# Second mixer: gate products on four quarters of the array, ScalarE in program order, one head left for the tile-by-tile end

## The chip, the core and the metric

The kernel runs on one core of a Trainium2 chip. The metric is the device time in microseconds of one execution. A core has TensorE (PE in the profile, its weight loads apart as PEld), VectorE (DVE), ScalarE (ACT), GpSimd (POOL) and SyncE (SP), each with a queue of its own that is worked off in order. SP's queue issues the DMAs of the weights. Matmuls write to PSUM; the other operands live in SBUF.

## The reference, cut to what matters

Two layers work on 256 context tokens and 256 latent tokens of width 1024: a half-step SwiGLU, a token mixer, a second half-step SwiGLU, each between RMS norms. The change is in the token mixer of the second layer, where only the latent tokens go on:

```
a, bx per head (64 channels) and direction d:
  r = sigmoid(xc @ w_r[d] + b_r[d]);  i = sigmoid(xc @ w_i[d] + b_i[d])
  a = exp(-8 r softplus(-lam));       bx = sqrt(1 - a^2) * (i * xc)
h = linear scan of (a, bx), context first, then latent; d = 1 runs backwards
o_lru = gelu(gate) * (h[0] + h[1])                      512 channels
o_sc  = b * conv3(c * x)                                256 channels
o_cm  = gelu(u) * (w_s @ gelu(v) + b_s)                 256 channels
x = x + mod * rms_norm(concat(o_lru, o_sc, o_cm) @ w_mix_out)
```

The 8 heads are taken two by two: a group c of 128 channels holds two heads, so there are four groups, 0 to 3.

## The kernel before

Channels lie on the 128 partitions, tokens along the free dimension: context tokens in columns 0 to 255, latent tokens in columns 256 to 511. A big product is made three times with operands split in two fp32r parts: `split` (line 169) makes the high part with a cast on ScalarE (L173) and the low part with a subtraction on VectorE (L174), in two halves for each weight unit. The weights come by `load_split` through 4 raw tiles; the high and the low parts have 6 tiles each.

`mixer` (line 630) runs once for each layer. In the second layer (`len(segs) == 1`) the string `ORDER[1]` says in which order its parts are issued. A part is a letter and a number, looked up in the table `parts` (line 846): `c`, `x`, `b` are the three projections of the short convolution; `g` a gate projection with its gelu; `u`, `v`, `m` the chunk mixing; `w` the load of a slice of the output weights; `C`, `G`, `D`, `S` the four steps of a group of LRU heads: convolution (`conv`, line 697: one ScalarE instruction, L701, and three on VectorE, L703), gates (`lru_gates`, line 712), decay (`lru_decay`, line 726: exp L730 and tanh L731 on ScalarE for each direction, then L732, L734, L735 on VectorE), scan (`lru_scan`, line 738: a square root on ScalarE, L741, for each direction, the rest on VectorE up to L751). `p` is the output product of slice m with the four short-convolution and chunk parts (k = 4 to 7).

Within the block at line 874 TensorE keeps the order of the program (`MANUAL`); the other engines' instructions are placed by the scheduler of the language, which may pull one ahead of another. A projection takes its weights from a queue that is loaded two units ahead (`unit`, line 675), so the two casts of a unit are issued two projections before its product.

`lru_gates` multiplies, for each direction, the block-diagonal 128x128 weights of two heads (half of them zeros) with all 512 columns of the group's convolution output: four fp32 products of 128x512 for each group, each in one PSUM bank. A sigmoid on ScalarE empties each bank (L719, L723). PSUM tiles named mm come from a pool of 6 banks (line 91), which go round.

The output product (`out_mm`, line 833) is plain fp32: for each slice m of 128 output channels it adds up eight products 128x256, k = 0 to 3 for the LRU groups, 4 to 7 for the others. `LATE` splits the LRU groups: for those of `LATE[0]` the products of all eight slices are made one group after the other (`out_part`, line 842); those of `LATE[1]` are made slice by slice at the end, and after each slice `tile_sums` (line 891) takes it up: three ScalarE instructions (L899 to L901) and a product and sums on VectorE and GpSimd, whose column sums TensorE makes with a vector of ones (tiles st). L934 reads them when all are done; the norm's scale and the next FFN follow. In this last part `MANUAL2` keeps the order of TensorE and VectorE; casts for the next FFN's weights (`pieces`) stand between the slices.

## Time and profile before

| | us |
|---|---|
| median of 3 runs (lowest, highest) | 1643.89 (1642.16, 1644.5) |
| the profiled execution | 1642.21 |
| its span, first to last instruction | 1640.4 |
| PE busy in it | 1612.5 (98%) |
| DVE busy | 1164.3 (71%) |
| ACT busy | 736.7 (45%) |
| POOL busy | 120.3 (7%) |

Times within the trace are microseconds from the span's start. The second mixer's parts run from about 1351 to 1439, so it is some 90 us of the whole. In a timeline row the first number is the start, the second the length from the start of the row's first instruction to the end of its last, and the bracket at the end is idle time of that engine just before, with what ended it. Instructions of an engine overlap a little, so the step from one to the next is shorter than one alone takes. The busy share of an engine over the whole run says little here, since the mixer uses the engines in other proportions than the FFNs around it.

### The profile page before, as it was taken

The page shows a single profiled execution, that of the slowest core. Times are in us where ns is not written, and L with a number is a line of the kernel's source. Part 1 is how long each engine was busy: PE and PEld are TensorE (multiplying, and loading weights), DVE is VectorE, ACT ScalarE, POOL GpSimd, SP SyncE. Part 2 cuts the span into 40 slices and gives each one's busy share as a digit, 9 for nine tenths or more (in the row PEclk, how much of TensorE's full clock was granted, in tenths as well). Part 3 has the DMA queues.
Part 4 walks back from the last instruction along what each step waited for, and adds up shares of the span by engine and source line. Part 5 has one row for each costly group of instructions (what it writes and reads, how often), then busy time and mean ns, then how long its engine had stood idle before and what let it go on. Part 6 is the DMA issues. An engine that isn't in the chain of part 4 may idle for free.

```text
span 1640.4 us, 23432 instructions
## 1 busy us (share of the span) xinstructions
PE 1612.5 (98%) x8846; PEld 1371.6 (84%) x8846; DVE 1164.3 (71%) x2183; ACT 736.7 (45%) x1378; POOL 120.3 (7%) x166
## 2 busy tenths in 40 slices
PE   6999999999999999999999999999999999999998
PEld 3788888889977998888888998888888998789997
DVE  4899898548788787867763887767432788785554
ACT  5523322244697662332233462332232479864543
POOL 0000000005000500000000410000000410100000
PEclk9999999999999999999999999999999999999999
DMA  9577677431323225655552215655422316155552
GB/s 370 189 218 261 205 229 223 144 121 44 103 72 120 77 97 187 221 162 174 179 164 80 100 61 194 222 166 167 141 90 90 103 54 210 47 167 194 180 191 78
DMA packets 73906, 249.97 MB, mean 152 GB/s; under 512 B 8384, under 2 KB 10048, under 8 KB 73792
## 3 DMA queue, kind: packets, MB, share of 16 engines
q1 hardware_dynamic: 73216, 247.94, 45.9%
q8 instruction: 69, 1.13, 0.3%
q10 hardware_dynamic: 576, 0.52, 0.1%
q14 instruction: 45, 0.37, 0.1%
HBM read 247.39 MB, written 1.05 MB: 151 GB/s over the span
## 4 chain that ended last, share of the span: by engine, by line
PE 89%; DVE 6%; ACT 3%; DMA 1%; issue 1%; POOL 0%; SPq 0%; POOLq 0%; DVEq 0%; ACTq 0%
PE mm L113 87%; PE st L113 1%; DVE x L271 1%; DVE sq L394 1%; DVE t L703 0%; PE mod L113 0%; DVE z L270 0%; DVE tmp L262 0%; DMA x<-in_xT 0%; ACT hi L173 0%; DVE t L397 0%; POOL rs L241 0%; DVE t L332 0%; DMA raw<-in_w_mi 0%; ACT t L730 0%
## 5 line engine op out<-in xcount | busy, mean ns | idle before, releaser
L173 ACT CAST hi<-raw 128x512 fp32r<-128x512 f32 (+1 forms) x596 | 343.6, 610 | 672.7 <-PE mm L113 475.8
L113 PE MATMUL mm<-hh,hi 128*128 128x512 f32 (+1 forms) x1840 | 625.6, 348 | 0.5 <-ACT hh L1095 0.2
L113 PE MATMUL mm<-hl,hi 128*128 128x512 f32 (+1 forms) x1840 | 622.5, 346 | 1.8 <-DVE hl L256 1.0
L174 DVE TENSOR_TENSOR lo<-raw,hi 128x512 fp32r<-128x512 f32 (+1 forms) x596 | 387.5, 680 | 157.3 <-ACT hi L173 154.5
L113 PE MATMUL mm<-hh,lo 128*128 128x512 f32 (+1 forms) x1840 | 466.6, 346 | 0.0
L113 PEld LDWEIGHTS mm<-hh,hi 128*128 128x128 f32 x1840 | 345.5, 188 | 52.1 <-ACT hh L1095 2.8
L113 PEld LDWEIGHTS mm<-hl,hi 128*128 128x128 f32 x1840 | 345.9, 188 | 51.2 <-DVE hl L1101 1.6
L113 PEld LDWEIGHTS mm<-hh,lo 128*128 128x128 f32 x1840 | 325.1, 188 | 47.2
L196 DVE SCALAR_TENSOR_TENSOR junk<-raw,cb 128x1024 bf16<-128x1024 f32 x256 | 312.9, 1222 | 70.8 <-DMA raw<-in_w_mod 67.1
L113 PE MATMUL mm<-t,hi 128*128 128x512 f32 (+1 forms) x1056 | 240.6, 367 | 0.0
L113 PEld LDWEIGHTS mm<-t,hi 128*128 128x128 f32 x1056 | 182.8, 188 | 35.7 <-issue 0.2
L397 POOL TENSOR_TENSOR t<-t,sq 128x256 f32<-128x256 f32 x112 | 94.2, 856 | 712.2 <-ACT sq L391 702.3
L113 PE MATMUL mm<-t,lo 128*128 128x512 f32 (+1 forms) x528 | 131.5, 367 | 0.0
L113 PEld LDWEIGHTS mm<-t,lo 128*128 128x128 f32 x528 | 92.6, 188 | 17.7
L480 DVE TENSOR_TENSOR sg<-sg,mm 128x512 f32<-128x512 f32 (+1 forms) x72 | 45.9, 640 | 78.3 <-PE mm L113 78.3
L113 PE MATMUL mm<-t,hh 128*128 128x256 f32 x512 | 71.2, 281 | 0.0
L113 PEld LDWEIGHTS mm<-t,hh 128*128 128x128 f32 x512 | 65.7, 188 | 0.5
L173 ACT CAST t<-sg 128x512 fp32r<-128x512 f32 (+1 forms) x94 | 50.6, 541 | 32.0 <-DVE sg L480 29.0
L332 DVE TENSOR_TENSOR t<-t,mm 128x256 f32<-128x256 f32 (+1 forms) x66 | 35.4, 536 | 29.3 <-PE mm L113 29.1
L174 DVE TENSOR_TENSOR t<-sg,t 128x512 fp32r<-128x512 f32 (+1 forms) x94 | 55.3, 589 | 0.9 <-ACT t L173 0.9
L113 PE MATMUL mm<-hi,t 128*128 128x512 f32 x176 | 55.1, 394 | 0.0
L263 ACT ACTIVATE hh<-tmp,modv 128x256 fp32r<-128x256 f32 x72 | 42.4, 596 | 22.1 <-DVE tmp L262 21.9
(179 smaller groups left out, 1212.4 us busy)
## 6 DMA issues: line engine op xcount, KB each, us to landing
raw<-in_w_in SPq DMA_DIRECT2D x176, 512.0 KB, 3.6
raw<-in_w_mod SPq DMA_DIRECT2D x128, 512.0 KB, 4.3
raw<-in_w_out SPq DMA_DIRECT2D x48, 512.0 KB, 3.3
raw<-in_w_mi SPq DMA_DIRECT2D x36, 512.0 KB, 4.1
raw<-in_w_last SPq DMA_DIRECT2D x22, 512.0 KB, 3.3
raw<-in_w_out SPq DMA_DIRECT2D x24, 384.0 KB, 3.7
t<-in_w_mod SPq DMA_DIRECT2D x32, 256.0 KB, 5.8
raw<-in_w_mo SPq DMA_DIRECT2D x8, 512.0 KB, 3.7
```

What stands on the lines that cost most here:

```text
L113: te.matmul(dst, lhsT=lhsT, rhs=rhs, start=start, stop=stop)
L173: sc.copy(hi, src)
L174: ve.tensor_tensor(lo, src, hi.bitcast(F32), op=OP.subtract)
L196: ve.scalar_tensor_tensor(junk, raw.rearrange("p k c -> p (k c)"), 1.0, cb[:, s], op0=OP.mult, op1=OP.mult, accum_out=modv[l][:, v, m, s:s ...
L263: sc.activation(hh[:, m, a:b], tmp, AF.Identity, scale=A, bias=B)
L271: ve.scalar_tensor_tensor(x[:, m, a:b], z, mcol(l, 3 * i + 2, m, s), x[:, m, a:b], op0=OP.mult, op1=OP.add)
L332: ve.tensor_tensor(y[m][:, a:b], y[m][:, a:b], p[:, :b - a], op=OP.add)
L394: ve.scalar_tensor_tensor(q[2], y, G, x[:, m, a:b], op0=OP.mult, op1=OP.mult)
L397: (gp if JACC[c] == "g" else ve).tensor_tensor(acc[c], acc[c], q[c], op=OP.add)
L480: ve.tensor_tensor(sg[:, :b - a], sg[:, :b - a], pu[:, :b - a], op=OP.mult)
```

## The change

Four things change, all in the second layer's mixer but for one name.

1. `lru_gates` works with 64x64 blocks. Each of the four products of a group becomes two products of 64 rows by 64 columns; the four that belong to one direction lie on the four quarters of the array. For this the convolution output is also needed with its two halves of partitions exchanged: `lru_swap` copies it with two DMAs of 128 KB from GpSimd's queue. The weights come in four small DMAs for a group instead of one of 256 KB. The first mixer keeps its products; its weight tile has another name.
2. ScalarE joins the engines that keep the program's order in the block of the parts.
3. `ORDER[1]` groups the parts by function.
4. `LATE` goes from `((0,), (1, 2, 3))` to `((1, 0, 3), (2,))`: groups 1, 0 and 3 are multiplied for all slices first, only group 2 is left for the slice-by-slice end.

```diff
-LATE = ((0,), (1, 2, 3))
+LATE = ((1, 0, 3), (2,))
...
-         "c0 x0 C1 C0 C3 C2 g3 g2 G1 G0 D1 D0 c1 b0 u0 v0 S1 w0 G3 u1 x1 b1 m1 w1 S0 m0 G2 w2 p1 w3 w4 w5 p2 p5 w6 D2 S2 w7 p0 "
-         "D3 S3 p7 p4 p3 p6")
+         "c0 x0 C1 C0 C3 C2 g3 g2 G1 G0 c1 b0 D1 D0 u0 u1 v0 S1 w0 S0 G3 G2 x1 b1 m1 m0 w1 w2 D3 D2 p1 w3 w4 w5 p2 p5 w6 S3 S2 w7 p0 "
+         "p7 p4 p3 p6")
...
+        def lru_swap(c):
+            t = turned_xc[c] = tp.tile([P, T], F32, tag="swap", name=nm("swap"), bufs=2)
+            for a, b in ((0, P // 2), (P // 2, 0)):
+                gp.dma_start(t[a:a + P // 2], xcs[c][b:b + P // 2])
+
+        def gate_products(c):
...
+            if len(segs) == 1:
+                wbd = tp.tile([P, 2, 2, P // 2], F32, tag="wbd", name=nm("wbd"))
+                for g in range(2):
+                    for h in range(2):
+                        a = 64 * h
+                        src = w_lru[l, c].rearrange("p (d g) o -> p d g o", g=2)
+                        nc.sync.dma_start(wbd[64 * g:64 * g + 64, :, h], src[a:a + 64, :, g, a:a + 64])
...
+            def products(d):
+                ps2 = pbank(), pbank()
+                for g, p in enumerate(ps2):
...
+                    for h in range(2):
+                        src = (xcs if g == h else turned_xc)[c]
+                        rows, cols = slice(64 * g, 64 * g + 64), slice(64 * h, 64 * h + 64)
+                        pe.matmul(p[cols], lhsT=wbd[rows, d, h], rhs=src[rows], start=True, stop=True)
+                return ps2
...
-                pr = pbank()
-                pe.matmul(pr, lhsT=wbd[:, 2 * d, :], rhs=xcs[c], start=True, stop=True)
+                pr, pi = products(d)
...
-        with tc.manual_schedule(engines=MANUAL):
+        with tc.manual_schedule(engines=MANUAL | {mybir.EngineType.Activation}):
```

What moves on the queues, at the three places that matter. First ScalarE, between the decays of groups 1 and 0 and the next gates (L730, L731 before are L764, L765 now; L805 is L839, the gelu of u; L798 is L832, the gelu of v; L741 is L775, the square root; L719 and L723, the sigmoids, are L755 and L757; L173 casts weights). Before:

```order
L805 ACT_TABLE_LOAD
L805 ACTIVATE t_12287<-mm_12262 128x256
L741 ACT_TABLE_LOAD
L741 ACTIVATE t_12125<-t_12125 128x512
L798 ACT_TABLE_LOAD
L798 ACTIVATE t_12330<-mm_12305 128x256
L741 ACT_TABLE_LOAD
L741 ACTIVATE t_12134<-t_12134 128x512
L798 ACT_TABLE_LOAD
L798 ACTIVATE t_12330<-mm_12332 128x256
L719 ACT_TABLE_LOAD
L719 ACTIVATE t_12373<-mm_12371,vec 128x512
```

and now, from the last instruction of the decays on:

```order
L765 ACTIVATE t_12182<-t_12182,s_100 128x512
L173 CAST hi_12282<-raw_12280 128x512 x2
L839 ACT_TABLE_LOAD
L839 ACTIVATE t_12313<-mm_12288 128x256
L173 CAST hi_12317<-raw_12315 128x512 x2
L839 ACTIVATE t_12348<-mm_12323 128x256
L173 CAST hi_12352<-raw_12350 128x512 x2
L173 CAST hi_12360<-raw_12358 128x512 x2
L832 ACTIVATE t_12391<-mm_12366 128x256
L832 ACTIVATE t_12391<-mm_12393 128x256
L775 ACT_TABLE_LOAD
L775 ACTIVATE t_12144<-t_12144 128x512
```

Fifteen table loads stand on ScalarE between the convolutions and the tile-by-tile end before, seven now. The casts of the two weight units of v (hi_12282 and hi_12317) now stand behind all eight instructions of the decays, and the square roots behind the second gelu of v.

Second TensorE, the gates of group 1 (wbd holds the gate weights, t_12031 the convolution output, swap its exchanged copy, each mm one PSUM bank). Before, four products, and the first of group 0:

```order
L113 MATMUL mm_12123<-t_12031,wbd_12121 128x512
L113 MATMUL mm_12127<-t_12031,wbd_12121 128x512
L113 MATMUL mm_12132<-t_12031,wbd_12121 128x512
L113 MATMUL mm_12136<-t_12031,wbd_12121 128x512
L113 MATMUL mm_12143<-t_12036,wbd_12141 128x512
```

Now on the same queue, with the swapped copy as one of the sources, all four of the first direction and the first of the second:

```order
L113 MATMUL mm_12138<-t_12031,wbd_12133 64x512
L113 MATMUL mm_12138<-swap_12036,wbd_12133 64x512
L113 MATMUL mm_12139<-swap_12036,wbd_12133 64x512
L113 MATMUL mm_12139<-t_12031,wbd_12133 64x512
L113 MATMUL mm_12149<-t_12031,wbd_12133 64x512
```

The second product of each group already needs the swapped copy. The gates of groups 3 and 2 now stand directly behind one another, eight banks in a row; before, five projections and a chunk mixing lay between them.

Third TensorE at the end (t_12134, t_12519 and t_12382 are the results of groups 1, 2 and 3 before; t_12461 and t_12488 those of groups 3 and 2 now; wo the output weights, one tile for each slice; c the product whose column sums st takes). Before:

```order
L113 MATMUL mm_12539<-t_12134,wo_12526 128x256
L113 MATMUL mm_12539<-t_12519,wo_12526 128x256
L113 MATMUL mm_12539<-t_12382,wo_12526 128x256
L113 MATMUL st_12635<-ones,c_12645 128x2 x2
L113 MATMUL mm_12539<-t_12134,wo_12533 128x256
L113 MATMUL mm_12539<-t_12519,wo_12533 128x256
L113 MATMUL mm_12539<-t_12382,wo_12533 128x256
L113 MATMUL st_12635<-ones,c_12651 128x2 x2
```

and now:

```order
L113 MATMUL mm_12639<-t_12461,wo_12633 128x256
L113 MATMUL mm_12592<-t_12488,wo_12428 128x256
L113 MATMUL mm_12592<-t_12488,wo_12564 128x256
L113 MATMUL mm_12603<-t_12488,wo_12566 128x256
L113 MATMUL st_12691<-ones,c_12697 128x2 x2
L113 MATMUL mm_12603<-t_12488,wo_12597 128x256
L113 MATMUL st_12691<-ones,c_12703 128x2 x2
L113 MATMUL mm_12644<-t_12488,wo_12599 128x256
```

Sixteen products, those of groups 1 and 3, have moved from between the slices to ahead of them. GpSimd has eight new entries, the DMAs of the swap; SP has twelve more small ones for the gate weights.

## Rows read from the trace of the kernel before

**Rows 1.** Busy time by stretch: length, PE, PEld, DVE, ACT, POOL, clock, DMA share, GB/s.

```profile
1352.00:1400.00 48.00, 47.77 (x330) 40.04 (x329) 40.51 (x71) 45.50 (x69) 0.00 (x0) 1.00 0.61 212
```

**Rows 2.** Groups of instructions on ACT by shape, 1352 to 1420: the table loads.

```profile
L741 ACT ACT_TABLE_LOAD x5 | 6.4, 1283 | 0.1
...
L719 ACT ACT_TABLE_LOAD x3 | 3.8, 1283 | 0.1
...
L730 ACT ACT_TABLE_LOAD x2 | 2.6, 1283 | 0.0
L805 ACT ACT_TABLE_LOAD x2 | 2.6, 1283 | 0.0
L798 ACT ACT_TABLE_LOAD x2 | 2.6, 1283 | 0.0
L731 ACT ACT_TABLE_LOAD x1 | 1.3, 1283 | 0.0
```

**Rows 3.** Timeline of PE around the last gates and the first output products.

```profile
1399.77 1.02 PE L113 MATMUL mm<-t,wbd 128*128 128x512 f32 x2
1400.63 1.03 PE L113 MATMUL mm<-t,wo 128*128 128x256 f32 x4
1401.88 17.53 PE L113 MATMUL mm<-t,wo 128*128 128x256 f32 x80 [0.23 <-DVE t L818]
1420.17 1.10 PE L113 MATMUL mm<-t,wo 128*128 128x256 f32 x4 [0.76 <-DVE t L751]
```

**Rows 4.** Timeline of DVE: the scan of the last group, and the end of the sums.

```profile
1415.32 1.28 DVE L742 TENSOR_TENSOR t<-t,t 128x512 f32<-128x512 f32 x2
...
1419.61 0.42 DVE L751 TENSOR_TENSOR t<-t,t 128x256 f32<-128x256 f32 x1
...
1438.94 0.16 DVE L934 TENSOR_SCALAR joint<-st 128x2 f32<-128x2 f32 x1 [1.04 <-PE st L113]
```

**Rows 5.** Groups by shape on PE, 1352 to 1439: the gate products.

```profile
L113 PE MATMUL mm<-t,wbd 128*128 128x512 f32 x32 | 14.3, 595 | 0.0
```

**Rows 6.** Timeline of PE at the kernel's start: products on four column quarters.

```profile
34.54 1.93 PE L113 MATMUL mod<-t,cs 128*32 128x512 f32 x16
```

**Rows 7.** Timeline of ACT: casts; a table load and what follows, sigmoids, exps.

```profile
1357.49 2.70 ACT L173 CAST hi<-raw 128x512 fp32r<-128x512 f32 x5
...
1381.47 1.28 ACT L741 ACT_TABLE_LOAD   x1
1382.77 0.63 ACT L741 ACTIVATE t<-t 128x512 f32<-128x512 f32 x1
...
1390.63 0.69 ACT L723 ACTIVATE t<-mm,vec 128x512 f32<-128x512 f32 x1
1391.20 0.69 ACT L719 ACTIVATE t<-mm,vec 128x512 f32<-128x512 f32 x1
...
1405.30 1.32 ACT L730 ACTIVATE t<-t,s 128x512 f32<-128x512 f32 x2
```

**Rows 8.** Timeline of DVE: the last six steps of the four convolutions.

```profile
1361.00 4.05 DVE L703 SCALAR_TENSOR_TENSOR t<-t,vec,t 128x512 f32<-128x512 f32 x6
```

**Rows 9.** DMA issues with KB each and us to landing; landing of the chunk weights.

```profile
wbd<-in_w_lru SPq DMA_DIRECT2D x8, 256.0 KB, 3.5
...
out<-t ACTq DMA_DIRECT2D x4, 128.0 KB, 1.8
...
DMA to landing us min/median/max: 2.7/5.1/7.5
```

**Rows 10.** Timeline of SP near the kernel's start.

```profile
45.01 0.42 SPq L714 DMA_DIRECT2D wbd<-in_w_lru  x1
55.22 0.33 SPq L179 DMA_DIRECT2D raw<-in_w_in  x1
```

**Rows 11.** ACT at the end: two neighbouring slices' first instructions; casts, 1420 to 1440.

```profile
1429.14 0.39 ACT L899 ACTIVATE t<-mm 128x256 f32<-128x256 f32 x1
...
1430.21 0.38 ACT L899 ACTIVATE t<-mm 128x256 f32<-128x256 f32 x1
...
L173 ACT CAST hi<-raw 128x512 fp32r<-128x512 f32 x6 | 3.6, 621 | 4.1 <-PE mm L113 4.1
```

**Rows 12.** Busy time by stretch, as Rows 1, during the norm's scale.

```profile
1438.00:1443.00 5.00, 4.75 (x23) 4.43 (x23) 3.02 (x12) 1.62 (x3) 2.29 (x2) 0.50 0.37 130
```

More of the change, by code (lines that the diff above doesn't have):

```diff
@@ L710, in lru_conv @@
             xcs[c] = conv(c)
+            if len(segs) == 1:
+                lru_swap(c)
+        turned_xc = {}
+        def lru_swap(c):
[3 more added lines that the diff above has]
+        def gate_products(c):
+            if len(segs) == 1:
+                wbd = tp.tile([P, 2, 2, P // 2], F32, tag="wbd", name=nm("wbd"))
[4 more added lines that the diff above has]
+                        nc.sync.dma_start(wbd[64 * g:64 * g + 64, :, h], src[a:a + 64, :, g, a:a + 64])
+            else:
+                wbd = tp.tile([P, 4, P], F32, tag="swap", name=nm("wbd"))
+                nc.sync.dma_start(wbd, w_lru[l, c])
+            def products(d):
+                ps2 = pbank(), pbank()
+                for g, p in enumerate(ps2):
+                    if len(segs) == 2:
+                        pe.matmul(p, lhsT=wbd[:, 2 * d + g, :], rhs=xcs[c], start=True, stop=True)
+                        continue
+                    for h in range(2):
[3 more added lines that the diff above has]
+                return ps2
+            return products
         def lru_gates(c):
-            wbd = tp.tile([P, 4, P], F32, tag="wbd", name=nm("wbd"))
-            nc.sync.dma_start(wbd, w_lru[l, c])
+            products = gate_products(c)
             for c, d, b in heads[2 * c:2 * c + 2]:
-                pr = pbank()
-                pe.matmul(pr, lhsT=wbd[:, 2 * d, :], rhs=xcs[c], start=True, stop=True)
+                pr, pi = products(d)
                 r = rs[c, d] = tt_()
                 sc.activation(r, pr, AF.Sigmoid, bias=V("b_r", b))
-                pi = pbank()
-                pe.matmul(pi, lhsT=wbd[:, 2 * d + 1, :], rhs=xcs[c], start=True, stop=True)
                 i = ix[c, d] = tt_()
```

## Prediction, made before the run

> **What bounds the kernel now.** I looked first at how busy each engine is in the stretch that changes. From 1352 to 1400 PE works 47.77 of 48 us and ACT 45.50, DVE 40.51 [rows 1]: two queues are full at once, so an us taken from one alone brings little. Next I asked what ACT does there. Fifteen table loads of 1.283 us, 19.3 us in all, stand among its instructions up to 1420 [rows 2]; they come because the scheduler mixes gelus, square roots and sigmoids. Then PE's timeline. The gates end, the first output product starts at 1400.63, 80 records run on without a gap from 1401.88, and the only real wait is 0.76 us, for L751, just before 1420.17 [rows 3]. That L751 is the last step of the last scan; it starts at 1419.61, and DVE had worked on that group's scan without a pause from 1415.32 [rows 4]. So in the old order the last scan is ready within an us of the moment when TensorE has done everything else. From there the tile-by-tile end takes until L934 at 1438.94 [rows 4]: 18.8 us. What follows L934 is the same work in both kernels, so L934 is where I take the sum.
>
> **The gates on quarters.** The 32 records of the gate products take 14.3 us of PE [rows 5]; 0.86 us lie between the starts of two gate records and the next product, 0.43 for one [rows 3], so sixteen products of two records cost 32 x 0.43 = 13.8. The change makes 32 products of 64 rows by 64 columns, 64 records. No row here shows two row halves at once. From below: if all four quarters run together, 64 / 4 x 0.43 = 6.9 us. From above: if only column parts run together, 64 / 2 x 0.43 = 13.8, no gain. The nearest row is that of products on four column quarters, 16 records in 1.93 us [rows 6], which is four at a time (4 x 0.43 and a tail). I take 6.9: PE is rid of 6.9 us.
>
> **ScalarE, alone.** Seven table loads instead of fifteen: 8 x 1.30 (load and the 0.02 to the next instruction, [rows 7]) = 10.4 us less on ACT. By the Trainium skill, page "ScalarE: Activation LUTs", section "What ACT_TABLE_LOAD costs", a switch costs a drain of some 1380 ns besides the load; here the next ACTIVATE starts 0.02 us behind the load [rows 7], so the row's price stands. By the page's price the four loads that lie before the new kernel's first square roots would put 4 x 1.38 = 5.5 us more on the sum below.
>
> **What this gives when the queues are followed.** I add up the rows along the three queues in the new order, each instruction behind its queue's last one and behind what it reads; casts step by 0.52 (five in 2.70, the last some 0.6 long), sigmoids by 0.57 and exps by 0.61 us [rows 7]. Done for the old order, the same addition gives 1438.3 for L934 where the trace has 1438.94, so I use the difference of two such sums. PE's work from the first gate (1362.5) to the last slices is known: 38.1 us from there to 1400.63 before, of which 13.8 gates, so 24.3 remain; with 6.9 of gates and 56 output products of 0.43 (80 records in 17.53 us, [rows 3]), 24.1, it is 55.3 us. Without a wait PE would be at the tile-by-tile end at 1417.8. These waits come on top:
>
> - The swap: 1.0. ACT now has to copy c's product before it starts the convolutions, and the first two end at about 1359.6 and 1361.7 (before, all but six steps were done by 1361.0, [rows 8]). PE is at group 1's gates at 1362.5. A swap lands 1.8 to 7.5 us after its issue by the nearest DMAs, 3.5 in the middle [rows 9]; I take 3.5, which leaves 0.6 for group 1 and 0.4 for group 0. At 1.8 nothing is left of it, at 7.5 it is 5. The later two swaps and the weights of those groups are due some 20 us before use. Of the twelve more loads on SP (0.33 to 0.42 each) eight stand near the kernel's start, where SP waits from 45.4 to 55.2 [rows 10]: nothing; without that cover they would cost some 3 us there.
> - The casts of v: 2.9. PE is through u1 at 1378.3. ACT, in order, has the sigmoids' load at 1363.0, eight sigmoids to 1368.9, four casts and a copy to 1371.2, a load, eight exps and tanhs (with 0.13 between the two of a pair, which work in place) to 1378.0, and only then the casts of v's first unit, a load, a gelu, and the casts of the second at 1381.6. DVE has the decays' twelve instructions ahead of the low parts. PE gets v's first low part at 1380.8 and its second unit's at 1381.8.
> - The banks of groups 3 and 2: 3.3. The second gelu of v comes at 1387.4; the four square roots and the load before the sigmoids stand behind it on ACT; the first sigmoid starts at 1392.3. PE fills six banks and waits for the first two to be emptied, until 1393.0. ScalarE empties a bank in 0.57 us [rows 7], the quarters would fill one in 0.43.
> - The output's start: 2.5. The scans of groups 1 and 0 can begin on DVE only with the square roots, at 1389.6 (before, at 1383.4); behind them come four products with sigmoids, the short convolution and the chunk mixing, which k = 5 to 7 of the first output product need: 1404.2.
>
> With 0.3 of small gaps this makes 10.0, and PE reaches the tile-by-tile end at 1427.6. The last scan is long done by then, at 1419.4.
>
> The Trainium skill has a rule that speaks against the change, page "TensorEngine Tiling (Array Packing)", section "PSUM Bottleneck": tiles speed up TensorE but not the emptying of PSUM. By it the gates would cost 16 x 0.57 = 9.2 us of PE and give 4.6, not 6.9; the third wait above, which I have from the rows alone, is of this kind.
>
> **LATE.** Before, 24 products lie between the slices' sums and take 24 x 0.43 = 10.3 us beside ACT's work. Now 8 do. The 16 others, 6.9 us, stand ahead of the end, and since PE comes there 8 us after the last scan, they fill no wait: they are time in which ACT has nothing to do. The end itself is then ACT's: a slice takes 1.07 [rows 11], six casts 0.5 each [rows 7], the copy of the norm's gain 0.5: 8.5 + 3.1 + 0.5 = 12.1 from 1428.2, then L903, the sums and L934: 1442.9, 15.3 us after PE's arrival instead of 18.8.
>
> **Sum.** 1442.9 against 1438.3 by the same addition over the old order: 4.6 us slower. Against the profiled execution, 1642.21 (1.8 around its span of 1640.4), that is 1646.8. The median of the runs shown, 1643.89, lies 1.7 above that execution, so I forecast 1648.5. What a measurement of this kernel can tell from no change is about 0.2%, 3.3 us.
>
> **Rivals.**
>
> 1. *Faster: nothing starves TensorE.* For it speak the 10.4 us freed on ACT and the 6.9 on PE, on the two queues that are full [rows 1]. If the casts of v are there when PE comes (ACT 3.3 us earlier than I add up) and the sigmoids keep pace with eight banks, PE comes to the end at about 1418.5, the scan is ready at about 1416, and L934 is at 1433.8: 4.5 us faster, 1639.4. It decides at the first low part of v: before 1378.3 it holds, at 1380.8 it falls. Against it: the order on ACT is fixed now, and 8 instructions of the decays stand there.
> 2. *No change that can be told:* the waits are there but some 3 us shorter in all, because I put a cast or a DVE row too late; 1645.5.
> 3. *Swaps land late.* At 7.5 us instead of 3.5 [rows 9] every later step moves by 4.0: 1652.5. GpSimd has issued no DMA in the trace, so I can't exclude it.
> 4. *The quarters don't do what they should:* the row halves run one behind the other. PE then needs 13.8 for the gates again; part of it falls into the bank wait, and the same addition gives 2.9 more: 1651.4.
> 5. *TensorE's clock falls.* Behind waits at the end of the old mixer it was granted 0.50 (1.2 GHz) from 1438 to 1443, after gaps of about an us [rows 12]. If the wait of 3.3 us at the banks does the same for 5 us, the projections in it take twice as long: 2.5 more, 1651.0.
>
> **How the numbers follow.** Forecast 0.48, rival 1 0.06, rival 2 0.22, rival 3 0.10, rival 4 0.08, rival 5 0.06. The forecast's own spread puts 0.03 of its 0.48 within 0.2%. So faster 0.06, same 0.22 + 0.03 = 0.25, slower 0.69. The range goes from 1643.0, rival 2 with most of the waits for v and for the output gone, to 1655.0, where rivals 3 and 5 come together; below lies rival 1, above only a swap that lands later than any DMA here.
>
> **What would show it.** Right: seven table loads in the second mixer; 64 gate records that start in fours about 0.43 us apart; PE waiting for a low part of v for 2 to 3 us, for sigmoids before group 2's second direction for about 3, for DVE behind the first output product; PE's first product of group 2 about 8 us after L751 of that group; ACT without gaps in the end and PE with them; L934 some 4 to 5 us later. Wrong: L751 of group 2 is what PE waits for at the end, then LATE pays and rival 1 has it; gate records 0.43 apart one or two at a time, rival 4; a long PE wait for the swap at group 1, rival 3; or a difference that lies outside 1352 to 1443.

## The result, and the profile after

| | before | after |
|---|---|---|
| median, us | 1643.89 (1642.16 to 1649.8, 5 runs) | 1656.07 (1653.84 to 1657.34, 5 runs) |
| profiled execution: span | 1640.4 | 1654.0 |
| granted clock over the span | 0.997 | 0.989 |

The changed kernel is slower: ratio 1.0068, 95% interval 1.0055 to 1.0082, 12.2 us between the medians. Forecast were 4.6 us and a range that ended at 1655.0. The side was right, the size was not, and the time lies outside the range.

**Where the time went.** Everything ahead of the second mixer is the same work in both kernels, so I count from its last common step, the last application of the norm on VectorE (tile tmp, L262), to the first reading of the sums (L934, now L968). Timeline of DVE, before and then after (start, length, engine, line, operation, and in brackets the idle time before it with what ended it):

```profile
1345.21 0.74 DVE L262 TENSOR_TENSOR tmp<-x,rb 128x256 f32<-128x256 f32 x2
```

```profile
1348.19 0.74 DVE L262 TENSOR_TENSOR tmp<-x,rb 128x256 f32<-128x256 f32 x2
...
1426.97 0.42 DVE L785 TENSOR_TENSOR t<-t,t 128x256 f32<-128x256 f32 x1
...
1453.45 0.16 DVE L968 TENSOR_SCALAR joint<-st 128x2 f32<-128x2 f32 x1 [1.61 <-PE st L113]
```

Before, the stage took 1438.94 - 1345.21 = 93.73 us [rows 4]; after, 1453.45 - 1348.19 = 105.26: **11.53 us more**. The remaining 3.0 us ahead of it and -0.9 behind it come from elsewhere (for the 3.0 see the last section). All numbers of the experiments below are in this frame: "at 61.07" means 61.07 us after that norm step of the same profile.

Busy time by stretch of the changed kernel (length; PE, PEld, DVE, ACT, POOL; granted clock, DMA share, GB/s), first the stretch that answers to [rows 1], then the end:

```profile
1355.00:1403.00 48.00, 42.51 (x312) 35.03 (x311) 38.56 (x66) 38.98 (x65) 4.30 (x8) 0.92 0.67 229
...
1440.00:1455.00 15.00, 14.24 (x60) 12.90 (x59) 8.99 (x23) 7.57 (x20) 3.86 (x4) 0.50 0.31 105
```

PE was busy for 47.77 of 48 us and is now for 42.51, at a lower clock; ACT went from 45.50 to 38.98, DVE from 40.51 to 38.56. All three have idle time now: each waits for another. In the end TensorE runs at 0.50, which is 1.2 GHz of 2.4. The table loads (groups on ACT by shape, 1355 to 1423) are seven, as in the order:

```profile
L755 ACT ACT_TABLE_LOAD x2 | 2.6, 1283 | 0.0
L764 ACT ACT_TABLE_LOAD x2 | 2.6, 1283 | 0.0
L775 ACT ACT_TABLE_LOAD x2 | 2.6, 1283 | 0.0
L839 ACT ACT_TABLE_LOAD x1 | 1.3, 1283 | 0.0
```

PE's timeline shows the waits:

```profile
1382.00 0.39 PE L113 MATMUL mm<-hi,hh 128*128 128x256 f32 x1 [0.40 <-ACT hi L173]
1384.10 0.38 PE L113 MATMUL mm<-lo,hh 128*128 128x256 f32 x1 [1.71 <-DVE lo L174]
...
1397.69 0.64 PE L113 MATMUL mm<-t,wbd 64*64 64x512 f32 x1 [3.24 <-ACT t L755]
...
1409.79 25.60 PE L113 MATMUL mm<-t,wo 128*128 128x256 f32 x116
...
1436.77 0.61 PE L113 MATMUL st<-ones,c 128*128 128x2 f32 x4 [1.38 <-DVE c L937]
1437.24 0.68 PE L113 MATMUL mm<-t,wo 128*128 128x256 f32 x2
```

The casts and the low part of v, then the banks of groups 3 and 2, then an output run of 116 records without a gap. It ends at 1435.39, 8 us after the last scan (L785 at 1426.97). ACT in the end:

```profile
1434.57 0.62 ACT L173 CAST hi<-raw 128x512 fp32r<-128x512 f32 x1 [14.77 <-PE mm L113]
1435.09 0.38 ACT L933 ACTIVATE t<-mm 128x256 f32<-128x256 f32 x1
...
1441.26 0.38 ACT L933 ACTIVATE t<-mm 128x256 f32<-128x256 f32 x1 [1.51 <-DVE c L937]
...
1445.11 0.39 ACT L933 ACTIVATE t<-mm 128x256 f32<-128x256 f32 x1 [0.59 <-PE mm L113]
...
1448.52 0.59 ACT L620 COPY t<-mm 128x512 f32<-128x512 f32 x1 [1.27 <-PE mm L618]
...
1449.63 0.49 ACT L935 ACTIVATE t<-mm,modv 128x256 f32<-128x256 f32 x1
```

ScalarE had nothing to do for 14.77 us, then needed 15.0 us for the eight slices (1435.09 to 1450.12). Of these it waited 1.51 us for VectorE and 0.59 and 1.27 for TensorE. Such waits were there in the end of the kernel before too; its eight slices took ScalarE 14.0 us (1422.18 to 1436.18). Timeline of ACT, before:

```profile
1428.14 0.38 ACT L899 ACTIVATE t<-mm 128x256 f32<-128x256 f32 x1 [1.12 <-DVE c L903]
...
1434.58 0.59 ACT L620 COPY t<-mm 128x512 f32<-128x512 f32 x1 [1.00 <-PE mm L618]
```

### The profile page after: what moved, and what is told of

The parts are those of the page before. It is cut to its first block, busy times and chain, and to the rows that moved or that the text cites. A ratio compares the mean times of both kernels' runs of the same rounds, so it can differ in the third digit from the quotient of the medians.

```text
span 1654.0 us, 23536 instructions
## 1 busy us (share of the span) xinstructions
PE 1620.9 (98%) x8878; PEld 1379.9 (83%) x8878; DVE 1163.6 (70%) x2183; ACT 726.0 (44%) x1370; POOL 124.8 (8%) x174
## 4 chain that ended last, share of the span: by engine, by line
PE 89%; DVE 5%; ACT 2%; issue 1%; DMA 1%; POOL 0%; SPq 0%; POOLq 0%; DVEq 0%; ACTq 0%
PE mm L113 87%; PE st L113 1%; DVE x L271 1%; DMA raw<-in_w_out 1%; DVE sq L394 1%; DVE lo L174 0%; DVE junk L196 0%; DVE z L270 0%; PE mod L113 0%; DVE tmp L262 0%; DMA x<-in_xT 0%; DVE t L397 0%; POOL rs L241 0%; ACT hi L173 0%; DVE t L332 0%
## 5 line engine op out<-in xcount | busy, mean ns | idle before, releaser
L173 ACT CAST hi<-raw 128x512 fp32r<-128x512 f32 (+1 forms) x596 | 343.6, 610 | 686.8 <-PE mm L113 493.7
L173 ACT CAST t<-sg 128x512 fp32r<-128x512 f32 (+1 forms) x94 | 50.6, 541 | 34.9 <-DVE sg L480 31.7
```

Source lines behind the costliest of these rows:

```text
L173: sc.copy(hi, src)
```

## The experiments

Theory at the outset: LATE carries the loss, because it takes work out of an end that does not get shorter, and TensorE's clock falls there. Rival: the waits for v and for the banks, that is ScalarE's fixed order, carry it. The table has each kernel's profile in the frame above (first output product; start of the last scan's last step; first column sum; L968), the difference of L968 to before, and the median of the runs with that of the kernel before on the same chip. Executions of one kernel differ by some us for reasons outside the mixer (last section), so a step of a mechanism is read from the frame, the verdict from the ratio.

| kernel | output | last scan | first sum | L968 | to before | median (before) | ratio, interval |
|---|---|---|---|---|---|---|---|
| before | 55.42 | 74.40 | 78.66 | 93.73 | | | |
| after | 61.07 | 78.78 | 88.58 | 105.26 | +11.53 | 1656.07 (1643.89) | 1.0068, 1.0055 to 1.0082 |
| late_old | 59.68 | 77.40 | 82.09 | 97.53 | +3.80 | 1645.24 (1644.71) | 1.0012, 1.0003 to 1.0021 |
| act_free | 62.01 | 80.12 | 89.52 | 106.20 | +12.47 | 1655.79 (1644.71) | 1.0075, 1.0061 to 1.0090 |
| full_gates | 59.31 | 77.03 | 88.03 | 104.70 | +10.97 | 1657.03 (1644.71) | 1.0082, 1.0067 to 1.0097 |
| quarters_only | 53.72 | 73.95 | 78.21 | 93.59 | -0.14 | 1644.38 (1644.71) | 0.9999, 0.9990 to 1.0008 |
| tail_warm | 59.73 | 77.46 | 88.88 | 104.16 | +10.43 | 1653.69 (1643.65) | 1.0061, 1.0047 to 1.0076 |
| late_on_before | 55.24 | 74.23 | 82.74 | 99.41 | +5.68 | 1649.99 (1643.65) | 1.0040, 1.0027 to 1.0052 |
| v_early | 58.66 | 76.37 | 81.05 | 95.48 | +1.75 | 1646.17 (1643.65) | 1.0008, 0.9996 to 1.0020 |
| cand_c | 57.40 | 75.07 | 79.76 | 94.18 | +0.45 | 1643.31 (1643.65) | 0.9996, 0.9984 to 1.0008 |
| gates_warm | 60.22 | 77.97 | 82.66 | 98.30 | +4.57 | 1647.82 (1644.30) | 1.0017, 1.0006 to 1.0028 |
| x1b1_early | 55.40 | 73.69 | 80.17 | 94.59 | +0.86 | 1647.90 (1644.30) | 1.0014, 1.0001 to 1.0026 |
| x1b1_casts | 51.64 | 72.27 | 80.56 | 94.98 | +1.25 | 1646.33 (1644.30) | 1.0008, 0.9998 to 1.0019 |
| x1b1_full | 54.83 | 72.71 | 80.68 | 95.10 | +1.37 | 1645.67 (1644.30) | 1.0008, 0.9999 to 1.0016 |
| m_early | 54.70 | 73.55 | 79.31 | 95.04 | +1.31 | 1645.25 (1644.01) | 1.0004, 0.9995 to 1.0013 |
| m_early_late | 51.48 | 72.02 | 78.59 | 95.26 | +1.53 | 1646.07 (1644.01) | 1.0012, 1.0000 to 1.0024 |
| m_early_full | 54.93 | 73.38 | 79.44 | 98.76 | +5.03 | 1650.62 (1644.01) | 1.0041, 1.0024 to 1.0057 |

One more difference has to be read from the table, for the clock fell for longer in the profiled execution of the changed kernel than in others. In after, late_old and tail_warm everything up to the first output product is issued alike, and the bank wait is 3.24 us in all three. Yet the output starts at 61.07 in after and at 59.68 and 59.73 in the others. Behind the wait the clock stayed low for longer in after (busy time by stretch, after and then tail_warm), and VectorE then waited for TensorE there (timeline of DVE, after), which it did not in late_old:

```profile
1397.50:1405.00 7.50, 7.31 (x30) 5.32 (x31) 7.50 (x14) 4.19 (x8) 0.00 (x0) 0.55 0.63 256
```

```profile
1394.50:1400.00 5.50, 5.43 (x27) 3.98 (x28) 5.50 (x11) 4.06 (x8) 0.00 (x0) 0.69 0.85 347
```

```profile
1405.51 0.42 DVE L807 TENSOR_TENSOR zl<-t,mm 128x256 f32<-128x256 f32 x1 [0.47 <-PE mm L113]
...
1408.34 0.42 DVE L817 TENSOR_TENSOR t<-t,mm 128x256 f32<-128x256 f32 x1 [0.92 <-PE mm L113]
```

These 1.4 us come neither from LATE nor from zeros at the end, which edit nothing ahead of the output; whether other executions of the changed kernel had them too, no profile shows. Counted from the first output product to L968, the kernels with one group left for the end take 43.8 to 45.4 us (after 44.19, act_free 44.19, late_on_before 44.17, tail_warm 44.43, m_early_late 43.78, full_gates 45.39); with three groups left and no long wait in that stretch it is 38.31 in the kernel before and 36.8 to 38.1 in late_old, v_early, cand_c and gates_warm.

### One part undone at a time

**late_old.**

```diff
-LATE = ((1, 0, 3), (2,))
+LATE = ((0,), (1, 2, 3))
```

> The changed kernel with LATE put back to ((0,), (1, 2, 3)); order, quarters and ScalarE's order stay as in the change. Theory A (LATE is the largest part of the loss: TensorE comes to the tile-by-tile end with too little work between the slices, waits 0.8 to 1.4 us for VectorE there, is granted 0.50 and the end takes 19.4 us although eight products are left of 24): with 16 products (6.9 us) back between the slices TensorE reaches the end about 6.9 us earlier, at 1427 in the changed kernel's time, when the last scan (1427.0) is just ready, and the end takes 18.8 us as in the kernel before: 6 to 8 us faster than the changed kernel, 1648 to 1650. Theory B (the waits for v and for the banks carry the loss, and the end is ScalarE's in both cases): under 3 us faster, 1653 to 1656.

Measured: 10.8 us under the changed kernel's median, which is more than theory A's 6 to 8, and 7.73 in the frame, of which 1.39 is the earlier start of the output and 6.34 comes behind it. Theory A, and B's "under 3" is out. PE and the stretch of the end in this kernel:

```profile
1427.03 0.61 PE L113 MATMUL st<-ones,c 128*128 128x2 f32 x4 [0.43 <-DVE c L937]
1427.49 1.54 PE L113 MATMUL mm<-t,wo 128*128 128x256 f32 x6
```

```profile
1425.00:1440.00 15.00, 13.12 (x79) 11.17 (x77) 9.22 (x20) 11.45 (x30) 4.12 (x5) 1.00 0.14 41
```

Six records of output products instead of two stand between the sums; the waits are 0.43 instead of 1.38, and the clock stays at 1.00. Counted from the output's start, the first sum comes 5.10 us earlier, since ten of the 16 products stand behind it now; from it to L968 it is 15.44 us, against 16.68 in the changed kernel, with these ten products (4.3 us of TensorE) more in it.

**act_free.**

```diff
-        with tc.manual_schedule(engines=MANUAL | {mybir.EngineType.Activation}):
+        with tc.manual_schedule(engines=MANUAL):
```

> The changed kernel with ScalarE left to the scheduler again; order, quarters and LATE stay. It has eleven table loads in the second mixer, against seven with the fixed order and fifteen before, and the casts of v's weights stand ahead of the decays. Theory A (the fixed order starves TensorE): the wait for v's low part (2.1 us) and the half clock behind it (1.7) go, the bank wait gets shorter: 4 to 6 us faster than the changed kernel, 1650 to 1652. Theory B (the order of the parts starves TensorE, not ScalarE's own): within 2 us of 1656, the four more loads (5.2 us) cost what the earlier casts give.

Measured: the changed kernel's time, theory B. The wait for v is gone, but with eleven table loads the gates wait three times (2.16 us, and the two below), and the clock falls behind them (0.50 from 1392 to 1404):

```profile
1394.08 1.11 PE L113 MATMUL mm<-swap,wbd 64*64 64x512 f32 x1 [2.25 <-ACT t L832]
...
1398.54 1.11 PE L113 MATMUL mm<-t,wbd 64*64 64x512 f32 x1 [2.49 <-ACT t L755]
```

Fixing ScalarE's order is neither the loss nor a gain.

**full_gates.** The quarters undone; the swap is not issued:

```diff
-            if len(segs) == 1:
-                lru_swap(c)
...
-                    if len(segs) == 2:
+                    if True:
```

> The changed kernel with the gates as 128x128 products without swaps, as before; all else stays. Theory A (quarters fill banks faster than ScalarE empties them, and the wait of 3.24 us and the half clock behind it, some 3.5, eat what they save): the gates of groups 3 and 2 take 3.4 us longer on TensorE, in place of that wait, and the clock may stay: the 3.4 us of groups 1 and 0 alone are lost, minus up to 3.5 of clock: 1654 to 1659. Theory B (quarters save their 6.9 us of TensorE in full): 6 to 7 us slower, 1662 to 1663.

Measured: theory A. In the frame it is 0.56 us faster than the change, by the median 1.0 slower, and the two ratios' intervals overlap. The bank wait ends in both kernels with the first sigmoids (at 1397.69 behind L755, which runs from 1396.95, in the change), and full gates need longer to fill the six banks ahead of it: the wait is 0.83 instead of 3.24, the clock stays at 1.00 to the end of the output products, and these start 1.8 us earlier. The 6.9 us that the quarters take off TensorE are worth nothing that can be told in this order.

**quarters_only.** The kernel before with `lru_swap` and the 64x64 products, all else as before.

> The kernel before with the quarters and swaps alone; order, LATE and ScalarE as before. Theory A (in the old order the last scan is ready within 0.8 us of TensorE, and ScalarE, full for 45.5 of 48 us, sets when): TensorE gets 6.9 us back and waits for it elsewhere: within 2 us of the kernel before, 1642 to 1646. Theory B (TensorE's time alone counts): 5 to 7 us faster, 1637 to 1639. Theory C (the waits bring the clock down as in the changed kernel): 2 to 5 us slower, 1646 to 1649.

Measured: no change, theory A (-0.14 us in the frame). The output products start 1.7 us earlier, and TensorE waits in the run for what is not ready; the last scan, which sets when the end begins, moves from 74.40 to 73.95.

### LATE, and the end

**late_on_before.** In the old order group 3 is the last scan, so it is the one left:

```diff
-LATE = ((0,), (1, 2, 3))
+LATE = ((0, 1, 2), (3,))
```

> The kernel before with LATE alone changed, to ((0, 1, 2), (3,)): three groups first, the group whose scan is last in the old order left for the end. Theory A (the 16 products moved ahead of the end are paid in full and the end does not get shorter, since it is not TensorE that sets it): 6.5 to 8 us slower than the kernel before, 1651 to 1653. Theory B (as predicted: the end becomes ScalarE's and 3.5 us shorter): 3 to 4 us slower, 1647.5 to 1648.5.

Measured: 6.3 us slower (4.4 to 8.5 by the interval), 5.68 in the frame. That lies between the two ranges, nearer theory A's. B fails by its mechanism: the end was to get shorter, and the way from the first sum to L968 is 16.67 us instead of 15.07. The first sum is 4.08 us later. So this one line lengthens both stretches, as in the changed kernel, without quarters, swaps or a new order:

```profile
1432.96 0.61 PE L113 MATMUL st<-ones,c 128*128 128x2 f32 x4 [1.38 <-DVE c L903]
1433.43 0.68 PE L113 MATMUL mm<-t,wo 128*128 128x256 f32 x2
```

```profile
1433.00:1448.00 15.00, 13.66 (x56) 11.76 (x56) 9.75 (x20) 9.90 (x26) 4.37 (x5) 0.57 0.23 71
```

**tail_warm.** Zeros added to each slice's sum, in the places where the old LATE had products:

```diff
             for m in range(KT):
...
+                for k in (1, 3):
+                    pe.matmul(out_bank(m), lhsT=zeros, rhs=oh[k][:, a0:b0], start=False, stop=False)
                 out_mm(m, LATE[1])
```

> The changed kernel, LATE as in the change, with two products of a zero matrix added to each slice of the tile-by-tile end (16 in all, 6.9 us of TensorE; they add zeros to the sum). Theory A (the end of the changed kernel is as long as the old one because TensorE has nothing to do between the slices and is granted 0.50 there; its own work does not set the end): with the dummies the granted clock stays at 1.00 until the last sums, as with LATE put back, and the time from the first column sum to L968 falls from 16.7 to about 15.4 us: 1 to 2 us faster than the changed kernel although TensorE does 6.9 us more. Theory B (TensorE's work sets the end, half clock or not): the dummies lengthen it by 3 to 7 us. Theory C (ScalarE and VectorE alone set it): within 0.5 us of the changed kernel.

Measured: 15.28 us from the first sum to L968 instead of 16.68, as theory A has it, with ten of the 16 dummies (4.3 us of TensorE) in that stretch:

```profile
1430.00:1446.00 16.00, 14.72 (x86) 12.56 (x84) 8.59 (x18) 12.37 (x31) 4.12 (x5) 1.00 0.11 33
1446.00:1453.00 7.00, 6.16 (x30) 5.83 (x31) 4.70 (x15) 1.65 (x4) 2.29 (x2) 0.57 0.51 155
```

The clock stays at 1.00 until the dummies are over. TensorE's work between the slices is free, and its absence costs 1.4 us. But six dummies stand ahead of the first sum, which comes 1.64 us later counted from the output's start, and so the whole way from there to L968 is 44.43 us against 44.19. The kernel as a whole is not shown to be faster: the 1.10 us less in the frame are the earlier start of the output, and the ratios' intervals overlap. Theory B's 3 to 7 us did not come; theory C's "within 0.5 us" fits the sum, though not the two stretches that it is made of.

### The rest: the new order

With LATE put back 3.8 us are left. These kernels build on late_old; the last two sets have a LATE of their own, given there.

**v_early.** Weight units are fetched four ahead, not two, from the second short convolution's first product to v:

```diff
-        def unit(ahead=2):
-            fill(ahead + 1)
+        deep = [2]
+
+        def unit(ahead=None):
+            fill((deep[0] if ahead is None else ahead) + 1)
...
         def short_c(q):
+            if len(segs) == 1 and q == 1:
+                deep[0] = 4
...
         def chunk_v():
+            deep[0] = 2
```

> The kernel with LATE put back (1645.2), with the weight units of the second short convolution's first product to u1 fetched and cast four ahead instead of two, so that the casts of v stand ahead of the decays on ScalarE. Theory A (the wait for v, 2.3 us in all, and the half clock behind it, 1.9, push everything behind): the output products start 3 to 4 us earlier, the last scan too, and the time falls by 2 to 4 us, to 1641 to 1643. Theory B (VectorE's work up to the last scan sets the time, so that the wait for v costs nothing): within 1 us of 1645.2.

Measured: the wait for v is gone, and TensorE waits longer for the next thing:

```profile
1394.38 0.87 PE L113 MATMUL mm<-t,wbd 64*64 64x512 f32 x1 [4.11 <-ACT t L757]
```

The output products start 1.0 us earlier, not 3 to 4. L968 comes 2.05 earlier; the other 1.0 is at its end, where the wait of L968 for the last sums was 1.42 us in late_old, whose clock was 0.51 there, and is 0.40 here. By the runs no difference can be told. Of 2.3 us of waiting and some 1.7 of half clock about 1 us was on the path to the output: nearer theory B.

**gates_warm.** The bank filled last before the wait is filled eight times:

```diff
-                    for h in range(2):
+                    for h in [0, 1] * (8 if (c, d, g) == (2, 0, 1) else 1):
```

> The kernel with LATE put back (1645.2), in which the last bank that TensorE fills before the bank wait of 3.24 us is filled eight times over instead of once (the products of that gate repeated, 7 more times 0.43 = 3.0 us), so that TensorE waits with work; ScalarE comes to that bank only about 2.3 us after the wait ends. Theory A (the half clock behind the wait, from 1394.6 to 1399, is paid for in full): the granted clock stays at 1.00 there, x1 and b1 run at full speed, the output products start about 2 us earlier and the time falls by about 2, to 1643. Theory B (VectorE, which works without a pause from 1391 to 1402 on scans and products, sets when the output products can start): they start at most 0.7 us earlier, and the time stays within 1 us of 1645.2.

Measured: the clock stays at 1.00, the output products come no earlier (60.22 against 59.68), nearer theory B. The median is 2.6 us above the 1645.2 from which B allowed 1, but the ratios (1.0017 and 1.0012) don't differ beyond their intervals. The dummies outlasted the wait by about 1.2 us, so the run does not price the half clock alone; but VectorE, without a pause, only came to the second short convolution's x1 at 57.2 and was through it at 59.1, and the chunk mixing still followed. Up to there VectorE waited for TensorE for 0.23 and 0.17 us, so at most 0.4 us could have been had.

**cand_c.** v_early, with the scans of groups 1 and 0 ahead of u and v:

```diff
-D1 D0 u0 u1 v0 S1 w0 S0 G3 G2
+D1 D0 S1 S0 u0 u1 v0 w0 G3 G2
```

> As the one with v's casts ahead, with the scans of groups 1 and 0 (S1 S0) moved ahead of u0 u1 v0, so that ScalarE takes their square roots right behind the decays and can take the sigmoids of groups 3 and 2 right behind v; still seven table loads. Theory A (VectorE's 5.5 us of waiting for the square roots in the changed kernel and the bank wait of 3.2 are both due to this order): bank wait under 1 us, output products start 4 to 6 us earlier than with LATE put back, the last scan is ready before TensorE needs it, the end starts at about 1416 to 1418: 5 to 7 us faster than 1645.2, that is 1638 to 1640 and 4 to 6 below the kernel before. Theory B (the last scan stays where it is, VectorE being full): within 2 us of the kernel before.

Measured: the time of the kernel before, 0.9996 (0.9984 to 1.0008). Last scan at 75.07, theory B. The bank wait did not shrink, since the gelus of u now stand behind the square roots, and the decays of groups 3 and 2 stand behind weight casts that wait for TensorE to be done with their buffers (ACT):

```profile
1390.39 0.64 PE L113 MATMUL mm<-t,wbd 64*64 64x512 f32 x1 [3.46 <-ACT t L844]
```

```profile
1400.43 1.14 ACT L173 CAST hi<-raw 128x512 fp32r<-128x512 f32 x2 [2.19 <-PE mm L113]
1403.27 1.14 ACT L173 CAST hi<-raw 128x512 fp32r<-128x512 f32 x2 [1.70 <-PE mm L113]
1404.42 1.28 ACT L766 ACT_TABLE_LOAD   x1
```

**x1b1_early, x1b1_casts, x1b1_full.** v_early with x1 and b1 between v and the gates, and LATE ((0,), (1, 3, 2)); then with one unit more cast ahead of the gates of groups 1 and 0 (`deep[0] = 3` at g2); then that with full gates:

```diff
-u0 u1 v0 S1 w0 S0 G3 G2 x1 b1 m1 m0 w1 w2 D3 D2 p1
+u0 u1 v0 x1 b1 S1 S0 w0 G3 G2 m1 m0 w1 D3 D2 w2 p1
```

> The kernel with v's casts ahead (unit fetched four ahead), with the order c1 b0 D1 D0 u0 u1 v0 x1 b1 S1 S0 w0 G3 G2 m1 m0 w1 D3 D2 w2 and then as in the change, LATE ((0,), (1, 3, 2)). Two projections (5.7 us of TensorE) now stand between v and the gates of groups 3 and 2, which gives ScalarE the time for its gelus, the four square roots and a table load; and the casts that held the decays D3 D2 back behind x1 and b1 (3.9 us of waiting) find their buffers free. Theory A (bank wait and late decays are the losses of cand_c): bank wait under 1 us, output products at 50 to 53 us after the norm's last step (before 55.4), last scan at 70 to 72 (before 74.4): 2 to 4 us below the kernel before, 1640 to 1642. Theory B (VectorE is full from the convolutions to the last scan): last scan at 74 or later, within 1.5 us of the kernel before.

> As x1b1_early, with one weight unit fetched and cast ahead of the gates of groups 1 and 0, where ScalarE waits 1.4 us for TensorE, instead of behind their sigmoids. Theory A: the decays D1 D0 begin about 1.5 us earlier, and so do their followers; 0 to 1.5 us faster than x1b1_early. Theory B (VectorE has to make the low parts in any case and is full): within 0.5 us of it.

> As x1b1_casts with the gates as 128x128 products without swaps. Theory A (with this order TensorE sets the start of the output products, so that the quarters' 6.9 us count): 3 to 7 us slower than x1b1_casts. Theory B (ScalarE's sigmoids and VectorE set it, quarters or not, as in the changed kernel, where quarters gave 0.6 us the wrong way): within 1 us of x1b1_casts.

Measured: x1b1_early fits neither theory: its last scan is at 73.69, short of both ranges, and its median is 3.6 us above the kernel before (0.86 in the frame). x1b1_casts is 1.6 us faster than it by the median and 0.4 slower in the frame, so that pair decides nothing. In x1b1_casts the gates of groups 3 and 2 no longer wait for sigmoids, and the last scan is ready 2.1 us earlier than before (72.27). Yet L968 is 1.25 us later than before, since the wait has moved:

```profile
1393.80 0.64 PE L113 MATMUL mm<-swap,wbd 64*64 64x512 f32 x1 [1.34 <-DVE t L823]
1402.83 22.36 PE L113 MATMUL mm<-t,wo 128*128 128x256 f32 x94 [5.01 <-DVE t L859]
```

TensorE begins the first output slice at 51.64 and then stands for 5.01 us before the chunk mixing's last product (L859), which VectorE takes only behind scans. That swallows what quarters give: with full gates the output starts 3.2 us later, the wait is 2.25, and the time is the same (theory B).

**m_early, m_early_late, m_early_full.** x1b1_casts with the mixing ahead of the scans, LATE ((1, 0), (3, 2)); then the change's LATE; then full gates:

```diff
-x1 b1 S1 S0 w0 G3 G2 m1 m0 w1
+x1 b1 m1 m0 S1 S0 w0 G3 G2 w1
```

> As x1b1_casts with the chunk mixing m1 m0 moved from behind the gates of groups 3 and 2 to between b1 and the scans S1 S0, so that VectorE takes its four instructions before the scans, and LATE ((1, 0), (3, 2)): two groups ahead of the end, two in it. Theory A (in x1b1_casts TensorE waits 5.0 us for the chunk mixing's last product, which stands behind two scans on VectorE; the last scan was ready 5 us before TensorE): that wait goes, the output products start at 50 to 51 us after the norm's last step, TensorE has its 48 products done at 71 to 72, when the last scan (72.3) is there, and L968 comes at 90.5 to 92 against 93.7 before: 2 to 3 us below the kernel before, 1641 to 1642.5. Theory B (VectorE's order only moves the wait: the last scan gets later by what the mixing takes): last scan at 73.5 or later, within 1 us of the kernel before.

> As m_early, with LATE as in the change, ((1, 0, 3), (2,)). Theory A (products moved out of the end are paid in full once TensorE comes behind the last scan, and the end runs at half clock): TensorE is 3.4 us later at the end with eight more products ahead, and the end loses 1.2 to 2.3 us to the clock: 3 to 6 us slower than m_early. Theory B (the products ahead of the end fill a wait for the last scan): within 1 us of m_early.

> As m_early with the gates as 128x128 products without swaps. Theory A (in this order nothing but TensorE sets the end, and the quarters' 6.9 us count at last): 3 to 6 us slower than m_early. Theory B (the last scan sets it): within 1 us of m_early.

Measured: m_early is 1.2 us above the kernel before by the medians, which its interval does not tell from nothing; the last scan is at 73.55, theory B. The 5.01 us are gone, and weight casts wait 3.42 us for their DMA on ACT, the gates 1.74 for a bank that VectorE empties. In the end the clock falls with 16 products between the slices (0.66 from 1425 to 1435):

```profile
1373.66 1.14 ACT L173 CAST hi<-raw 128x512 fp32r<-128x512 f32 x2 [3.42 <-DMA raw<-in_w_mi]
```

```profile
1395.53 0.64 PE L113 MATMUL mm<-swap,wbd 64*64 64x512 f32 x1 [1.74 <-DVE t L823]
```

```profile
1425.00:1435.00 10.00, 9.51 (x39) 7.50 (x38) 5.73 (x12) 6.00 (x18) 3.95 (x5) 0.66 0.15 55
```

m_early_late costs 0.2 us in the frame and 0.8 by the medians of twelve runs each, not 3 to 6: theory B's numbers. In the profile this has a cause other than B's. Its output products start 3.2 us earlier (51.48; in that execution the weight casts waited 2.09 us for their DMA and the gates 1.19, and the clock did not fall behind them, as it did to 0.66 from 1395 to 1400 in m_early), and from there to L968 it takes 43.78 us against 40.34, 3.4 more for eight products. LATE edits nothing ahead of the output, so this start would be chance; that the medians agree as well is not explained by two profiles.

m_early_full is 5.4 us slower than m_early by the medians, 3.7 in the frame, and the two ratios' intervals lie apart: by the runs quarters pay in this order, as theory A has it. But not by its mechanism. The output products start at 54.93 and the last scan is at 73.38, as in m_early: the difference lies wholly behind the first sum, where TensorE was granted 0.54 from 1425 to 1443 (0.75 in m_early) and the end took 19.3 us instead of 15.7. Why the clock fell deeper there stays open. No version beat the kernel before beyond its interval.

## Why the prediction was right and wrong

**Right: side, place, and most of the mechanism up to the end.** The gates run four at a time: groups 1 and 0 took 4.35 us (1365.63 to 1369.98) where I put 3.45. There are seven table loads. The first ACTIVATE behind one starts at its end (1366.14 + 1.28, 1367.43), and the load itself starts 0.02 us behind the instruction ahead of it (1366.12 and 1366.14). So nothing here shows the drain of some 1380 ns that the Trainium skill, page "ScalarE: Activation LUTs", section "What ACT_TABLE_LOAD costs", adds to a load. The row's price of 1.30 held. The swaps landed in 2.2 to 4.6 us, 2.6 in the middle, where I took 3.5; TensorE's products waited for none (one weight load did, 0.3 us), so the 1.0 us for them was not there. The wait for v was 2.1 us with 2.9 forecast, the bank wait 3.24 with 3.3. TensorE comes to its first product of group 2 some 7 us behind the last scan, with 8 forecast. The page "TensorEngine Tiling (Array Packing)" of the Trainium skill, section "PSUM Bottleneck", says that tiles speed up TensorE and not the emptying of PSUM. The trace agrees: the wait for the banks ends with the first sigmoids, which quarters don't bring forward, and full_gates takes it from 3.24 to 0.83 and loses nothing that can be told.

**The step that failed: "The end itself is then ACT's".** I made the end 15.3 us instead of 18.8 by adding ScalarE's instructions without gaps (12.1) and 2.6 for the sums, and put its waits at nothing without a reason. TensorE's first product of group 2 starts at about 1434.1 (three products of 0.43 ahead of 1435.39), L968 at 1453.45: 19.4 us. ScalarE took 15.0 from its first slice to its last. Its instructions alone came to 11.7 of that; the rest were the waits, 1.51 us for VectorE, whose step on the slice ahead stood behind two low parts of the next weights (at 1441.26), and 1.86 for TensorE. The sums came 3.3 us behind the last slice, at half clock. The old end, whose trace I had, shows the same two waits (1.12 and 1.00 us in the rows of before above): ScalarE took 14.0 us for the slices there, more than 12.1, with the clock at 1.00 up to 1435. So the 6.9 us moved ahead of the end were paid, and the 3.5 that I let the end give back were not there. Counted from the first output product LATE costs 6.3 us in the new order and 5.9 in the old one; in my sum it had 3.4.

**The clock, half seen.** Rival 5 had it once, at the bank wait, for 2.5 us and a chance of 0.06. It fell three times: behind the wait for v (0.57 from 1384.8 to 1388.6, about 1.6 us), behind the bank wait (0.52 from 1398 to 1405, about 3.4) and through most of the end. With the first two the output started at 61.07 and not at the forecast 59.0 (1404.2), and they took the place of the 2.5 us of waiting for it, of which nothing was left (PE busy for 5.00 us from 1405 to 1410). Part of that is this execution's: in late_old and tail_warm the second fall was shorter and the output came at 59.7. In the end the clock is worth 1.4 us by tail_warm. I had read the fall behind the old end [rows 12] and did not ask what TensorE would do in an end from which two thirds of its products were taken.

**The sum again.** 6.9 us more than forecast in the mixer: about 3.5 because TensorE reached the end at 85.9 and not at 82.4, 4.1 because the end was 19.4 and not 15.3, less the 0.6 by which my addition was short for the old order too. (The waits add up to 1427.8, where I wrote 1427.6; that 0.2 changes nothing.)

**Rivals.** The first fell at its own condition (v's low part came at 1384.1, 1381.1 in the frame of before). Rivals 3 and 4 did not occur. The largest part was in none of them: it is the term for the end, which I had with the wrong sign. Of rival 5 the mechanism came, in more places than the one that I gave it.

**What stays open.** Why fixing one wait always met another is shown only as far as it went: in the kernel before VectorE is at work for 60.1 of the 68 us from 1352 to 1420 (40.51 of 48 [rows 1], then the row below), and no order tried here brought the last scan below 72. Whether one could, with VectorE's order fixed too, was not tried. Busy time of the kernel before:

```profile
1400.00:1420.00 20.00, 19.19 (x86) 15.88 (x84) 19.59 (x35) 16.22 (x23) 0.00 (x0) 1.00 0.00 1
```

## What to carry to other kernels

Before work is moved out of a closing part, ask what that part waits for. Here products between other engines' steps cost nothing, cost their time ahead of the end where no wait was left to fill, and kept TensorE's clock up (24 of them did, and 8 with 16 of zeros; 16 in m_early did not). An end is not as long as its busiest engine's instructions; read the waits between its engines in the end that exists. Where two or three queues are full together, a saving on one is worth what the next wait leaves of it, so follow a new order to the second and third wait before it is believed.

## What was not expected of the hardware

Work that is the same, instruction by instruction, took 1344.8 to 1350.2 us up to the last norm step in the profiles of these kernels. The steps are of about 1.5 to 2 us, at the norms near 955 and 1330 and in some profiles near 410. Busy time by stretch, before and then after:

```profile
955.00:960.00 5.00, 5.00 (x45) 5.00 (x44) 3.86 (x16) 1.07 (x3) 1.41 (x2) 1.00 0.64 212
1330.00:1335.00 5.00, 5.00 (x45) 5.00 (x44) 3.55 (x15) 1.30 (x4) 1.41 (x2) 1.00 0.68 213
```

```profile
955.00:960.00 5.00, 5.00 (x34) 5.00 (x33) 2.54 (x12) 0.28 (x2) 1.41 (x2) 0.70 0.65 211
1330.00:1335.00 5.00, 5.00 (x31) 5.00 (x31) 3.46 (x14) 1.18 (x3) 1.40 (x2) 0.66 0.58 157
```

Behind the same small gaps ahead of the same products (4.80 of 5 us busy from 950 to 955 in both) the clock fell in one execution and not in the other. That is the 3.0 us ahead of the mixer. It is probably much of the spread between runs of one kernel too: of 23 runs of the kernel before on one chip the fastest took 1641.06 us at a mean granted clock of 0.997, the slowest 1648.99 at 0.992; profiles of those runs there are none. And products of zeros made a stretch of the end shorter: with ten of them, 4.3 us of TensorE, it took 15.28 us instead of 16.68.
